# Seven-product units of a split-precision FFN: two units in a row share one tile for a quarter of their weights, and the later units' sums lie in the tile of the conditioning vectors

## The chip, the cores and the metric

One core of a Trainium2 chip runs the whole program in one launch. The time is device microseconds (us); three runs of the kernel before gave 1621.66, 1622.32 and 1625.24 us, median 1622.32.

## What is computed

The reference is a two-layer transformer over 256 latent and 256 context tokens, width 1024, in float32. The change touches its half feed-forward blocks (FFN, inner width 2816) and the vectors that modulate them:

```python
def half_ffn(h, shift, scale, gate, w_in, w_out, g, b):
    xm = modulate(h, shift, scale)
    a, u = jnp.split(xm @ w_in, 2, axis=-1)
    y = (jax.nn.silu(a) * u) @ w_out
    return post_norm(h, 0.5 * gate * y, g, b)

mod_lat = jnp.split((jax.nn.silu(c) @ ada_w[i] + ada_b[i])[:, None, :], N_MOD, axis=-1)
mod_ctx = jnp.split((jax.nn.silu(c_ctx) @ ada_w[i] + ada_b[i])[None, None, :], N_MOD, axis=-1)
```

Four such blocks are computed: first FFN of layer 0, attention, second FFN of layer 0, first FFN of layer 1, mLSTM, second FFN of layer 1. The change touches the second and third of the four.

## The kernel before

**Number format.** Every float32 operand of a matrix product is split into a high and a low part of type fp32r: `split` (lines 225 to 231) copies the value on ScalarE (ACT, line 226) into the high part, and VectorE (DVE, line 231) subtracts it from the value for the low part. `mm3` (line 240) then issues three matmuls, high by high, high by low, low by high; its `mm` is line 242 in the profile.

**Units.** The first product of an FFN, `w_in`, is done in 22 units of 128 columns of `a` and 128 of `u`. A plain unit streams 512 tokens through 16 weight blocks: 48 matmuls of 512 columns. In the two FFNs concerned (`FAST`, entries 1 and 2), units 9 to 21 are done by `fast_in` (line 643) with seven products of 2 by 2 blocks in place of eight: each product is 4 blocks deep and 256 tokens wide, so a unit is 84 matmuls of 256 columns. Its weights come by two DMAs of 512 KB (`raw`, line 211): `r0` holds the quarters a11 and a21, `r1` holds a12 and a22. DVE makes four sums s1 = a21 + a22, s2 = s1 + a11, s4 = s2 + a12, s3 = a11 + a21 (line 651), each 128 by 512, and `split` makes their high and low parts. The products run in the order a11, a12, s1, s2, a22, s4, s3. Between them ACT copies partial results out of PSUM (lines 676, 679, 681, 683): product 4 adds onto the bank that line 676 copies, product 6 onto that of line 679, product 7 onto that of line 681. At a unit's end come the sum at line 685, the Silu on ACT (line 686), lines 689 and 690 on DVE, and the split of the result into the unit's two tiles `gh`, `gl`.

**Order.** An FFN has two halves. Half 0 is units 0 to 10, then 8 output units (`unit_out`) that multiply by `w_out`; half 1 is units 11 to 21, then the other half of the outputs, of which the first four come ahead of the next norm. Each output unit is 33 matmuls of 512 columns, over eleven `gh`, `gl` pairs in their order, so the pair of unit 21 is read last. With the outputs run the dots that make the modulation vectors of later blocks: `ada_load` (line 353) fetches a row block of `ada_w`, `ada_dot` (line 359) multiplies it on DVE by both vectors silu(c), silu(c_ctx), 1220 ns each. These two vectors lie, repeated in all 128 partitions, in the tile `cb` of 2 by 1024 (`silu_c`, `silu_load` at line 306, `silu` at line 315). In the units 9 to 21 nothing reads `cb`; the output units of both halves do.

**Buffers.** Raw weights rotate through 3 tiles (`RAW`), split weights through 7 tiles of tag `w` (`WB`), each of which holds a high and a low part of 1024 columns; sums and other temporaries rotate through 6 tiles of tag `tmp`. A seven-product unit takes four `w` tiles, of which the first holds only the quarter a11 and stays half empty, and six `tmp` tiles: s1, s2, s4, s3 and its `a`, `u`.

**What sets the order on each engine.** The program is written in Python order; the framework's scheduler places the instructions of each engine in a fixed sequence of its own when the program is built, and adds the semaphores. Instructions passed through `pin` keep their written order. `fast_in`, `split`, `silu_load` and `silu` (as called here) are not pinned. All weight loads and the loads of `cb` are issued on SP's queue, one behind the other.

Of the kernel before, what the change touches and what calls it, by code (L numbers as in the profile page):

```python
# [27 lines left out]
NFH = 11  # L28
# [5 lines left out]
SH = 16  # L34
# [138 lines left out]
class Body:  # L173
# [75 lines left out]
    def x(self, d, g):  # L249
        return self.xh[:, d, g[0] : g[1]], self.xl[:, d, g[0] : g[1]]  # L250
# [350 lines left out]
    def fast_operands(self):  # L601

        self.flush()
        self.shut()
        self.cp = None
        st = self.open()
        n = ND // 2 * TL
        x = self.t([P, 6 * n], F32R, pool=st)
        self.t([P, FLIP], pool=st)
        self.made = [[x[:, (2 * i + p) * n : (2 * i + p + 1) * n].rearrange("p (k f) -> p k f", f=TL) for p in range(2)] for i in range(3)]  # L610
        self.first = {}

    def fast_sums(self, i):

# [28 lines left out]
    def fast_in(self, j, w_in, sh):  # L643

        nc, V, S = self.nc, self.nc.vector, self.nc.scalar
        half = 4 * P
        r0, r1 = (self.raw(w_in[2 * j + i]) for i in range(2))
        part = lambda x, i: x[:, i * half : (i + 1) * half]
        a11, a21, a12, a22 = part(r0, 0), part(r0, 1), part(r1, 0), part(r1, 1)
        s1, s2, s4, s3 = (self.tmp() for _ in range(4))  # L650
        add = lambda o, x, y: V.tensor_tensor(out=o, in0=x, in1=y, op=ALU.add)  # L651
        ws = [self.pair(sh=sh, n=half)] + [self.pair(sh=SH) for _ in range(3)]
        self.split(a11, *ws[0])
        self.split(r1, *ws[1])
        add(s1, a21, a22)
        add(s2, s1, a11)
        add(s4, s2, a12)
        add(s3, a11, a21)
        for i, x in enumerate((s1, s2, s4, s3)):
            self.split(x, *(part(y, i % 2) for y in ws[2 + i // 2]))  # L660
        w = {n: [part(x, i) for x in ws[p]] for n, p, i in (
            ("a11", 0, 0), ("a12", 1, 0), ("a22", 1, 1), ("s1", 2, 0), ("s2", 2, 1), ("s4", 3, 0), ("s3", 3, 1),
        )}
        of = lambda k0, g: lambda k: self.x(k0 + k, g)
        made = lambda i: lambda k: [x[:, k, :] for x in self.made[i]]

        def product(o, name, x, first, last):
            for k in range(ND // 2):
                c = slice(k * P, (k + 1) * P)
                self.mm3(o, [y[:, c] for y in w[name]], x(k), first and k == 0, last and k == ND // 2 - 1, group=False)  # L670

        x, yv, z = self.mm()[:, :TL], self.mm(), self.mm()[:, :TL]
        y, v = yv[:, :TL], yv[:, TL:]
        a, u = self.tmp(), self.tmp()
        product(x, "a11", of(0, LAT), True, False)
        S.copy(a[:, :TL], x)
        product(y, "a12", of(ND // 2, LAT), True, True)
        product(v, "s1", of(0, CTX), True, False)
        S.copy(u[:, TL:], v)
        product(x, "s2", made(0), False, False)  # L680
        S.copy(a[:, TL:], x)
        product(z, "a22", made(2), True, True)
        S.copy(u[:, :TL], z)
        product(v, "s4", of(ND // 2, CTX), False, True)
        V.tensor_tensor(out=a, in0=a, in1=yv, op=ALU.add)
        S.activation(a, a, AF.Silu)
        product(x, "s3", made(1), False, True)
        u2 = u.rearrange("p (n f) -> p n f", n=2)
        V.scalar_tensor_tensor(u2, x[:, None, :].broadcast_to([P, 2, TL]), -1.0, u2, ALU.mult, ALU.subtract)
        V.tensor_tensor(out=a, in0=a, in1=u, op=ALU.mult)  # L690
        gh, gl = self.gt[j] = tuple(self.t([P, self.gw], F32R, tag=k, bufs=self.gn, pool=self.gp) for k in ("gh", "gl"))
        self.split(a, gh, gl)

    def ffn(self, layer, s, gate, groups, side, start=None):
# [4 lines left out]
        with self.tc.tile_pool(name=f"ffn{li}", bufs=1) as gp:  # L699
# [6 lines left out]
            def unit_in(j, w, g, steps={}, ks=range(ND), ps=None):  # L706
                n = g[1] - g[0]
                pa, pu = ps or (self.mm(), self.mm())
                for k in ks:
                    for part, o in ((0, pa), (1, pu)):  # L710
                        self.mm3(o[:, :n], w(part_k(part, k)), self.x(k, g), k == 0, k == ND - 1)
                    self.steps(steps.get((j, k), ""))
                if ks[-1] < ND - 1:
                    return pa, pu
                self.ffn_g(j, pa, pu, g)
# [18 lines left out]
            for hf in range(2):  # L734
                js = list(range(hf * NFH, (hf + 1) * NFH))[0 if hf else done :]
                if hf == 0 and not start:
                    first = js[:LEAD]
                    ws = {j: Keep(self, [w_in[2 * j + i] for i in range(2)], lambda c: SH if c else SHR) for j in first}
                    assert len(self.running) == 1

                    k0, k1 = range(ND // 2), range(ND // 2, ND)
                    for j in first[:-1]:
                        unit_in(j, ws[j], LAT, LEADSTEP[li])
                    j = first[-1]
                    ps = unit_in(j, ws[j], LAT, ks=k0)
                    assert not self.running
                    pc = unit_in(first[0], ws[first[0]], CTX, ks=k0)
                    ws[j](ND)
                    unit_in(first[0], ws[first[0]], CTX, ks=k1, ps=pc)
                    unit_in(j, ws[j], LAT, ks=k1, ps=ps)  # L750
                    for j in first[1:]:
                        unit_in(j, ws[j], CTX)
                    for j in first:
                        call("in", j)
                    js = js[LEAD:]
                fast, sums = FAST[li]
                for j in js:
                    if j >= fast:
                        self.fast_in(j, w_in, SHR if j in (fast, NFH) else SH)
                    else:  # L760
                        unit_in(j, stream(j), allg)
                        if j >= LEAD + FAFTER:
                            self.fine = False
                    assert not self.running
                    if j <= sums:
                        call("in", j)
                    self.residual(2, self.pin)
                    if j == sums:
                        self.fast_operands()
                    if sums <= j < sums + 2:  # L770
                        self.fast_sums(j - sums)
                    if j == fast - 1:
                        self.fast_first()
                if not hf:
                    self.residual(len(self.later))
                w = Stream(self, [w_out[hf * NFH + i] for i in range(NFH)], lambda c, hf=hf: SHR if hf and c == (ND - TAIL) * NFH // ND else 0)
                body = ND - TAIL if hf else ND
                self.halves = []
                if hf and fast < NF:
                    self.shut()  # L780
                    self.cp = self.open()
                for d in range(body):
                    unit_out(hf, d, w, allg)
                    call("out", hf, d)
                self.halves = []
                if body < ND:
                    w = Keep(self, w.chunks, SH, w)
                    self.fine = True
                    for g in groups:
                        for d in range(body, ND):  # L790
                            unit_out(hf, d, w, g, TAILSTEP)
                            self.flush()
                    self.steps('B')
# [994 lines left out]
```

## Time and profile before

| | |
|---|---|
| runs | 1621.66, 1622.32, 1625.24 us; median 1622.32 us |
| the profiled execution's own time | 1621.19 us |
| its span, first to last instruction | 1619.4 us |
| mean granted TensorE clock | 0.999 |
| matmuls | 10424 |

The span is what the views below divide; 1.8 us of the execution's own time lie outside it. The profiled execution is 1.1 us under the median of the runs. Times in the views are us from the span's start.

### The profile page before, as it was taken

What the parts mean: (1) busy time and instruction counts of PE and PEld (TensorE: products, weight loads), DVE (VectorE), ACT (ScalarE), POOL (GpSimd) and SP (SyncE); (2) the same over time, 40 slices, a digit from 0 to 9 for tenths busy, and PEclk for the clock granted to TensorE, in tenths of its full rate; (3) what the DMA queues carried; (4) which work ended last, traced back from release to release, by engine and by line L of the source; (5) the groups of instructions that cost most, each with busy time, mean ns of one, the idle gap of its engine ahead of it and who ended that gap; (6) DMA issues with size and microseconds to landing.
All of it is one profiled execution on the core that took longest, in us unless ns stands there. A gap on an engine that the chain in (4) does not pass through costs nothing. (4 is left out here: it accounts for less than half of the span.)

```text
span 1619.4 us, 26945 instructions
## 1 busy us (share of the span) xinstructions
PE 1602.0 (99%) x10424; PEld 1452.0 (90%) x10424; DVE 1377.6 (85%) x2783; ACT 760.0 (47%) x1344; POOL 62.2 (4%) x77
## 2 busy tenths in 40 slices
PE   9999999999999999999999999999999999999998
PEld 7888888889988998889998998889999989999987
DVE  7789989878879879889996977789978968897697
ACT  6522132324676343515661444426642657566542
POOL 0000000001011200000000100000001000020000
PEclk9999999999999999999999999999999999999999
DMA  9667777642203343453254240752363332437552
GB/s 360 219 218 224 260 228 242 207 142 86 66 1 94 116 142 93 177 175 105 105 179 159 80 144 26 264 191 105 122 226 135 123 105 92 147 102 260 179 176 90
DMA packets 71648, 249.49 MB, mean 154 GB/s; under 512 B 7896, under 2 KB 10712, under 8 KB 71520
## 3 DMA queue, kind: packets, MB, share of 16 engines
q1 hardware_dynamic: 70944, 246.99, 46.2%
q8 instruction: 81, 1.33, 0.3%
q10 hardware_dynamic: 576, 0.79, 0.1%
q14 instruction: 47, 0.39, 0.1%
HBM read 246.69 MB, written 1.05 MB: 153 GB/s over the span
## 5 line engine op out<-in xcount | busy, mean ns | idle before, releaser
L242 PE MATMUL t<-t,t 128*128 128x256 f32 (+2 forms) x8484 | 1302.4, 314 | 5.5 <-DVE t L231 1.7
L242 PEld LDWEIGHTS t<-t,t 128*128 128x128 f32 x8484 | 1176.8, 188 | 117.0 <-DVE t L231 2.5
L226 ACT CAST t<-t 128x1024 fp32r<-128x1024 f32 (+4 forms) x573 | 436.4, 785 | 462.6 <-PE t L242 144.1
L231 DVE TENSOR_TENSOR t<-t,t 128x256 fp32r<-128x256 f32 (+3 forms) x792 | 516.5, 690 | 100.3 <-ACT t L226 98.5
L359 DVE SCALAR_TENSOR_TENSOR t<-t,t 128x1024 bf16<-128x1024 f32 x224 | 260.5, 1220 | 0.2 <-DMA t<-in_ada_w 0.2
L597 ACT ACTIVATE t<-t 128x256 f32<-128x256 f32 (+1 forms) x67 | 32.1, 485 | 108.9 <-PE t L242 107.9
L946 PE MATMUL t<-t,t 128*128 128x256 f32 (+1 forms) x256 | 79.5, 311 | 0.1
L948 PE MATMUL t<-t,t 128*128 128x256 f32 (+1 forms) x256 | 78.7, 307 | 0.1
L947 PE MATMUL t<-t,t 128*128 128x256 f32 (+1 forms) x256 | 78.3, 306 | 0.0
L728 DVE SCALAR_TENSOR_TENSOR t<-t,t,t 128x256 f32<-128x256 f32 x96 | 42.7, 478 | 32.3 <-PE t L242 32.2
L493 POOL TENSOR_TENSOR t<-t,t 128x256 f32<-128x256 f32 x30 | 23.0, 768 | 1106.4 <-ACT t L483 1105.0
L874 PE MATMUL t<-t,t 128*128 128x512 f32 (+1 forms) x300 | 60.5, 364 | 0.0
L874 PEld LDWEIGHTS t<-t,t 128*128 128x128 f32 x300 | 51.5, 189 | 8.9
L598 DVE TENSOR_TENSOR t<-t,t 128x256 f32<-128x256 f32 (+1 forms) x67 | 36.3, 545 | 25.5 <-ACT t L597 19.5
L651 DVE TENSOR_TENSOR t<-t,t 128x512 f32<-128x512 f32 x78 | 53.6, 687 | 3.0 <-DMA t<-in_ffn_in 2.2
L1475 PE MATMUL t<-t,t 128*128 128x512 f32 (+2 forms) x276 | 55.4, 356 | 0.0
L1475 PEld LDWEIGHTS t<-t,t 128*128 128x128 f32 (+1 forms) x276 | 44.9, 183 | 10.5 <-issue 0.4
L483 ACT ACTIVATE t<-t 128x256 f32<-128x256 f32 x72 | 26.3, 411 | 56.2 <-DVE t L476 56.2
L946 PEld LDWEIGHTS t<-t,t 128*128 128x128 f32 x256 | 48.4, 189 | 3.0 <-ACT t L550 0.3
L948 PEld LDWEIGHTS t<-t,t 128*128 128x128 f32 x256 | 48.1, 188 | 2.8 <-DVE t L551 0.3
L947 PEld LDWEIGHTS t<-t,t 128*128 128x128 f32 x256 | 48.1, 188 | 2.6
L550 ACT ACTIVATE t<-t,t 128x256 fp32r<-128x256 f32 x72 | 32.8, 502 | 30.1 <-DVE t L549 30.1
(209 smaller groups left out, 1117.5 us busy)
## 6 DMA issues: line engine op xcount, KB each, us to landing
t<-in_ffn_in SPq DMA_DIRECT2D x168, 512.0 KB, 4.0
t<-in_ada_w SPq DMA_DIRECT2D x138, 512.0 KB, 4.4
t<-in_ffn_out SPq DMA_DIRECT2D x66, 512.0 KB, 4.6
t<-in_ffn_last SPq DMA_DIRECT2D x22, 512.0 KB, 3.6
t<-in_att_in SPq DMA_DIRECT2D x12, 512.0 KB, 3.8
t<-in_att_out SPq DMA_DIRECT2D x8, 512.0 KB, 3.5
t<-in_ml_qk SPq DMA_DIRECT2D x8, 512.0 KB, 3.9
t<-in_ml_v SPq DMA_DIRECT2D x8, 512.0 KB, 4.0
```

What stands on the lines that cost most here:

```text
L226: self.behind(self.nc.scalar.copy(h, x))
L231: self.behind(self.nc.vector.tensor_tensor(out=ls, in0=xs, in1=hs.bitcast(F32), op=ALU.subtract))
L242: mm = lambda *k, **kw: self.nc.tensor.matmul(*k, skip_group_check=not group, **kw)
L359: ins = nc.vector.scalar_tensor_tensor(self.tmp().bitcast(BF16), r, 1.0, self.cb[:, v, :], ALU.mult, ALU.mult, accum_out=to)
L598: V.tensor_tensor(out=sl, in0=sl, in1=pu[:, :n], op=ALU.mult)
L651: add = lambda o, x, y: V.tensor_tensor(out=o, in0=x, in1=y, op=ALU.add)
L728: V.scalar_tensor_tensor(z, y[:, gg[0] - t0 : gg[1] - t0], gate()[:, v, d : d + 1], z, ALU.mult, ALU.add)
L874: pin(nc.tensor.matmul(o, gs[g], ws[k][w][:, i : i + n], start=k == k0 and g == w == 0, stop=k == k1 - 1 and g == 1,))
L946: mm(o, self.xh[:, k, c], wh, start=k == 0, stop=False)
L947: mm(o, self.xh[:, k, c], wl, start=False, stop=False)
L948: mm(o, self.xl[:, k, c], wh, start=False, stop=k == ND - 1)
L1475: mm = lambda *k, **kw: pin(nc.tensor.matmul(*k, **kw))
```

## The change

Three things are done in the two FFNs with seven-product units.

- Two units in a row share one `w` tile for their quarter a11: units 9 and 10, 11 and 12, 13 and 14 and so on; unit 21 opens one and uses half of it. The tile is kept in a list `quarter`.
- From unit 11 on, s1, s2, s4, s3 are written into `cb`, which has room for exactly four 512-column sums, in place of four `tmp` tiles; `split` is called twice, on 1024 columns each (s1 with s2, s4 with s3), in place of four times on 512.
- Behind unit 21 `cb` is loaded again and the Silu is applied again, ahead of the outputs of half 1.

```diff
-        self.first = {}
+        self.first, self.quarter = {}, []
...
-        s1, s2, s4, s3 = (self.tmp() for _ in range(4))
+        late = j >= NFH
+        sums = self.cb.rearrange("p v d -> p (v d)")
+        s1, s2, s4, s3 = (part(sums, i) if late else self.tmp() for i in range(4))
         add = lambda o, x, y: V.tensor_tensor(out=o, in0=x, in1=y, op=ALU.add)
-        ws = [self.pair(sh=sh, n=half)] + [self.pair(sh=SH) for _ in range(3)]
+        if not self.quarter:
+            p = self.pair(sh=sh)
+            self.quarter = [[part(x, i) for x in p] for i in range(2)]
+        ws = [self.quarter.pop(0)] + [self.pair(sh=SH) for _ in range(3)]
         self.split(a11, *ws[0])
         self.split(r1, *ws[1])
         add(s1, a21, a22)
         add(s2, s1, a11)
         add(s4, s2, a12)
         add(s3, a11, a21)
-        for i, x in enumerate((s1, s2, s4, s3)):
-            self.split(x, *(part(y, i % 2) for y in ws[2 + i // 2]))
+        if late:
+            for i in range(2):
+                self.split(self.cb[:, i, :], *ws[2 + i])
+        else:
+            for i, x in enumerate((s1, s2, s4, s3)):
+                self.split(x, *(part(y, i % 2) for y in ws[2 + i // 2]))
...
                 if hf and fast < NF:
                     self.shut()
                     self.cp = self.open()
+                    self.silu_load()
+                    self.silu()
```

## Rows read from the trace of the kernel before

**Rows 1.** The page, busy time of each engine over the span.
```profile
PE 1602.0 (99%) x10424; PEld 1452.0 (90%) x10424; DVE 1377.6 (85%) x2783; ACT 760.0 (47%) x1344; POOL 62.2 (4%) x77
```

**Rows 2.** Busy time by stretch: units 9-10, units 11-21, outputs; then the other FFN.
```profile
core 0: us, PE busy (x) PEld busy (x) DVE busy (x) ACT busy (x) POOL busy (x), PEclk, DMA share, GB/s
656.20:677.40 21.20, 20.01 (x170) 19.54 (x169) 19.22 (x31) 15.14 (x30) 0.00 (x0) 1.00 0.45 147
...
737.30:842.30 105.00, 105.00 (x926) 104.81 (x925) 100.62 (x152) 69.96 (x131) 0.00 (x0) 1.00 0.37 127
842.30:872.00 29.70, 29.70 (x134) 24.54 (x133) 21.27 (x48) 8.91 (x11) 0.00 (x0) 1.00 0.63 229
1007.30:1027.50 20.20, 19.78 (x170) 19.34 (x169) 19.09 (x30) 15.11 (x30) 0.00 (x0) 1.00 0.48 152
1087.40:1192.30 104.90, 104.90 (x926) 104.77 (x925) 100.79 (x152) 70.14 (x132) 0.00 (x0) 1.00 0.37 129
```

**Rows 3.** TensorE by stretch: units 12, 14, the other FFN's 12, then two equal stretches.
```profile
746.94:756.46 9.52, 9.52 (x87) 1.00 0.34 114
...
765.98:775.74 9.76, 9.76 (x87) 1.00 0.33 112
...
1097.04:1106.73 9.69, 9.69 (x87) 1.00 0.38 117
...
661.80:668.20 6.40, 6.40 (x56) 1.00 0.41 157
790.00:796.40 6.40, 6.40 (x59) 1.00 0.37 112
```

**Rows 4.** Groups by line and shape, units 9 and 10, 656.2 to 677.4 us.
```profile
L242 PE MATMUL t<-t,t 128*128 128x256 f32 x168 | 20.2, 280 | 1.2 <-DVE t L231 1.1
...
L651 DVE TENSOR_TENSOR t<-t,t 128x512 f32<-128x512 f32 x5 | 3.4, 687 | 1.6 <-DMA t<-in_ffn_in 1.6
```

**Rows 5.** ACT in order of time, units 13 and 14, 764 to 778 us.
```profile
768.80 1.05 ACT L226 CAST t<-t 128x1024 fp32r<-128x1024 f32 x1 [0.70 <-DMA t<-in_ffn_in]
769.76 0.36 ACT L676 COPY t<-t 128x256 f32<-128x256 f32 x1
...
775.12 1.15 ACT L226 CAST t<-t 128x512 fp32r<-128x512 f32 x2
```

**Rows 6.** DVE in order of time, the same stretch.
```profile
764.88 1.89 DVE L231 TENSOR_TENSOR t<-t,t 128x512 fp32r<-128x512 f32 x3
...
771.63 1.41 DVE L651 TENSOR_TENSOR t<-t,t 128x512 f32<-128x512 f32 x2
773.00 0.69 DVE L231 TENSOR_TENSOR t<-t,t 128x512 fp32r<-128x512 f32 x1
773.61 0.69 DVE L651 TENSOR_TENSOR t<-t,t 128x512 f32<-128x512 f32 x1
```

**Rows 7.** Groups by line and shape, units 11 to 21, 737.3 to 842.3 us.
```profile
L231 DVE TENSOR_TENSOR t<-t,t 128x512 fp32r<-128x512 f32 x64 | 42.2, 686 | 0.0
L226 ACT CAST t<-t 128x512 fp32r<-128x512 f32 x63 | 38.0, 622 | 15.5 <-DVE t L651 13.8 <-DVE t L690 0.7
...
L231 DVE TENSOR_TENSOR t<-t,t 128x1024 fp32r<-128x1024 f32 x14 | 17.1, 1222 | 1.5 <-ACT t L226 1.3
L226 ACT CAST t<-t 128x1024 fp32r<-128x1024 f32 x15 | 15.8, 1051 | 6.7 <-DMA t<-in_ffn_in 4.3 <-DMA t<-in_ffn_out 2.4
```

**Rows 8.** DVE in order of time, start of unit 11.
```profile
735.46 1.42 DVE L651 TENSOR_TENSOR t<-t,t 128x512 f32<-128x512 f32 x2
```

**Rows 9.** Sources 315 and 306: ACT's idle time ahead of the Silu; the vectors' landing.
```profile
  DMA t<-in_c: 12.7, 1
...
DMA to landing us min/median/max: 3.8/4.3/4.7
```

**Rows 10.** ACT in order of time, end of unit 21.
```profile
841.50 1.05 ACT L226 CAST t<-t 128x1024 fp32r<-128x1024 f32 x1 [2.07 <-DMA t<-in_ffn_out]
```

**Rows 11.** DVE in order of time, the last low parts of unit 21 among pieces of `w_out`.
```profile
846.86 2.03 DVE L231 TENSOR_TENSOR t<-t,t 128x256 fp32r<-128x256 f32 x5
```

## The prediction, made before the kernel was run

> **What bounds the kernel now.** First the page's busy times: TensorE (PE) is busy 99% of the span, VectorE (DVE) 85%, ScalarE (ACT) 47% [rows 1]. A busy PE says little alone, so next come the stretches with seven-product units, at a granted clock of 1.00 throughout, the 2.4 GHz level [rows 2]. One undisturbed unit takes 9.52 us [rows 3], 113.3 ns for each of its 84 matmuls, and eleven of them make 104.7 us; units 11 to 21 take 105.0 us in one FFN and 104.9 in the other [rows 2]. So at most 0.3 and 0.2 us of waiting lie in the stretch where the change does most. Units 9 and 10 have 21.2 and 20.2 us [rows 2] where two undisturbed units take 19.04: 2.2 and 1.2 us lost. All that this change could win where it acts, at PE's present pace, is thus 3.3 + 0.5 = 3.8 us, 0.23% of the time. I take 0.2%, 3.2 us, as what a measurement of this kernel can tell from no change.
>
> Then what the other engines do there. DVE is busy 100.6 of 105.0 us in units 11 to 21, 96%, ACT 70.0 [rows 2]: the feed of weights is close behind PE, and what it does on time matters more than how much.
>
> **Part 1: four splits of 512 become two of 1024 (units 11 to 21).** By busy time DVE saves 4 x 686 - 2 x 1222 = 300 ns a unit and ACT 4 x 622 - 2 x 1051 = 386 ns [rows 7]; over 22 units 6.6 and 8.5 us. The instructions overlap their neighbours, so less of it is room: three subtractions of 512 take 1.89 us in a row, some 0.60 each [rows 6]. None of it lies on PE's path as long as PE waits for none of these parts, so I cost it at nothing. The cover is that the splits run a unit ahead.
>
> What does wait on the feed is small. In unit 14 PE loses 9.76 - 9.52 = 0.24 us, in the other FFN's unit 12 0.17 [rows 3]. The cause shows on ACT: the 1024-wide copy of a raw tile waits 0.70 us for its DMA, and behind it on ACT stands the copy of line 676, from 769.76 to 770.12 [rows 5]. Product 4 adds onto that bank; it is due three products into unit 14, 765.98 + 3 x 1.36 = 770.06. That copy comes 0.06 late, plus the hand-over. The DMA was late because its raw tile comes free only when DVE has made the sums, and DVE puts a subtraction, 0.6 us, between the sums s2 and s4 [rows 6]. With 1024-wide splits that subtraction cannot start until ACT has copied s1 and s2 together, 1.05 us, so the four sums should follow each other; the raw tile then comes free some 0.6 us earlier in every unit, and both waits should go: -0.4 us. If the scheduler puts the 1.22 us subtraction there instead, the tile is free 0.5 us later and the waits stay or grow; I take -0.4 with 0 as the other end here and price the worse end with the slower rival.
>
> The new cost is that s1 is ready only with s2. It bites at unit 11, which has no unit of the same kind ahead. Its first two sums are ready at 735.46 + 1.42 = 736.9 [rows 8]; a copy of 1.05 and a subtraction of 1.22 [rows 7] put the low part at 739.2; product 3 needs it at 737.4 + 2 x 1.36 = 740.1. If the other two sums and the two output sums of line 728 go ahead on DVE (some 2.1 us), it is 1.1 us late. Bounds 0 and +1.1 in each FFN; I take +0.1 each, near the end without a wait, since DVE must stand idle for ACT's 1.05 us anyway and can do two of those four in it.
>
> The Trainium skill (Perfetto Trace Analysis, Optimizing Scalar/DVE Operations) says that large operations help a saturated engine, but that if ACT or DVE is not saturated and causes bubbles elsewhere, breaking instructions up lets work finish sooner. By its second half the merge would cost at unit 11 what the upper bound says, 2.2 us in all; by its first half, with DVE at 96%, nothing. I go by the rows' 0.9 us of room.
>
> **Part 2: the sums lose their rotating tiles.** They now lie in one place, so a unit's sums must wait for the last unit's splits. Before, the splits of unit 14's sums stand on DVE at 764.88 for 1.89 us and the next unit's first sum at 771.63 [rows 6]: 4.9 us between. No wait, 0 us. [...] At unit 11 the sums must also follow the last dot that reads the vectors; both are on DVE, where the sums come behind the dots already.
>
> **Part 3: the shared quarter.** Two units take seven `w` tiles in place of eight. In units 9 and 10 PE waits 1.1 us, and that for a DVE subtraction; DVE in turn waited 1.6 us for a weight DMA [rows 4]. A free `w` tile mends neither, and these units keep their `tmp` sums. So 0, with bounds -3.3 (all waits there go) and 0. The other side: a new pair's tile is held until the first product of the pair's second unit ends.
>
> **Part 4: the vectors are made again.** Per FFN two DMAs on SP and two Silus on ACT, beside two waits: the DMAs wait for unit 21's last split, and all weight loads stand behind them on SP; the Silus wait for the DMAs, and the copies of unit 21 stand behind them on ACT. The same load ahead of this FFN landed 4.3 us after issue, and ACT stood 12.7 us idle for it [rows 9], at a place where PE did not need ACT. Two 1024-wide ACT instructions cost 2 x 1.05 = 2.1 us [rows 7]. At the end of unit 21 ACT is idle 2.07 us in one piece, for a DMA [rows 10]: room for both. If they land badly, the last pair `gh`, `gl` is late: outputs start at 842.3, at 29.70/134 = 0.22 us a matmul [rows 2], and the low part is read by the 32nd, at 849.2; the DVE group that holds it ends at 848.9 [rows 11]. So 0.3 us of slack at least, and a bound of 2.1 - 0.3 = 1.8 us per FFN from work alone. The weight loads have more cover: a 1024-column chunk feeds 24 matmuls, 5.3 us. Bounds 0 and +1.8 each; I take +0.1 each, by the idle 2.07 us. The dots that need the vectors come after the first output unit, 33 x 0.22 = 7.3 us later, against 4.3 + 2.1 = 6.4 us for load and Silu.
>
> **Sum.** -0.4 + 0.2 + 0 + 0 + 0.2 = 0.0 us on the profiled execution's 1621.2; its own runs' median lies 1.1 us higher, so the forecast is **1622.3 us**, no change.
>
> **Rivals.**
> *Faster: the waits of units 9 and 10 go as well,* because a freed `w` tile or another order on DVE brings the sums of unit 10 early. For it: 3.3 us are really lost there. Against: the wait shown is for a DMA. Time: 1622.3 - 3.3 - 0.4 = 1618.6.
> *Slower: PE falls into its slower pace in units 11 to 21.* After the waits in unit 9, 56 matmuls fit in 6.40 us where 59 fit in an undisturbed stretch, with no wait between [rows 3]: 5% slower, and it lasted until the next wait. If a wait in unit 11 or 12 leaves PE so, ten units lose 0.05 x 9.52 = 0.48 us each, 4.8 us in one FFN. Against: after the waits of units 12 and 14 the next stretch is at full pace (59 in 6.40). It decides where s1's low part misses 740.1 or line 676's copy its time. Time: 1627.
> *Slower: the reload holds ACT.* ACT reaches the first Silu before the DMA has landed and stands there. Price: 2.1 us of work and up to 4.3 - 2.07 = 2.2 of waiting, less 0.3: 4.0 at most, some 1.5 to 2 us likely, per FFN. It decides where the Silu stands ahead of line 683's copy or of the copy into `gh`. Time: 1625.3 to 1626.3, or inside 0.2% if one FFN is spared.
> *The sharing makes a wait of its own.* The copy of a later unit's a11 is made early: it is one of the two copies at 775.12 to 776.27 [rows 5], while unit 15's first product ends at 775.74 + 1.36 = 777.1. If it must wait for that, ACT stands 0.8 to 1.4 us in every second unit, and line 676 is late as in unit 14: 0.3 to 0.5 us in ten units, 1626. Other `w` tiles are free at that time, which speaks against it.
>
> **How the numbers follow.** Forecast 0.66 (all within 0.2%); faster 0.08; pace 0.08; reload 0.12, half of it past 0.2%; sharing 0.06. Faster by over 0.2%: 0.08; within: 0.66 + 0.06 = 0.72; slower: 0.08 + 0.06 + 0.06 = 0.20. The range takes in the reload and the sharing, and leaves out most of the two outer cases: 1619.2 to 1626.5.
>
> **What would show it.** Right: in units 11 to 21 two 1024-wide copies and subtractions per unit in place of four of 512; the four sums in one block on DVE; 104.7 us for each eleven units; units 9 and 10 at 21 and 20 us; two more Silus at line 315 per FFN with PE at full pace at the start of the outputs. Wrong: a PE wait in unit 11 on the 1024-wide subtraction; fewer than 59 matmuls in 6.40 us anywhere in units 11 to 21; idle ACT ahead of line 315 with PE waiting behind it; units 9 and 10 near 19 us.

## The result, and the profile after

The changed kernel is **slower**: median 1628.08 us (1623.85 to 1629.53, 9 runs) against 1621.25 us before (1620.02 to 1625.24, 9 runs), ratio 1.0035 with interval [1.0025, 1.0046]. The forecast of no change was wrong, and the median lies past the end of the range, 1626.5 us. The profiled execution took 1629.53 us, the slowest of its nine; its span is 1627.7 us, 8.3 more than before.

The page first, for [rows 1]:

```profile
span 1627.7 us, 26880 instructions
...
PE 1608.3 (99%) x10424; PEld 1456.5 (89%) x10424; DVE 1372.0 (84%) x2739; ACT 755.0 (46%) x1304; POOL 62.3 (4%) x77
```

DVE has 44 instructions and 5.6 us less, ACT 40 and 5.0 us, as the merge of the splits said. PE has the same 10424 matmuls and is busy 6.3 us longer, at the same granted clock. So less was done, and it took longer. The stretches say where (columns as in [rows 2], and the same stretches):

```profile
657.10:678.90 21.80, 20.10 (x170) 19.50 (x169) 18.73 (x30) 14.67 (x29) 0.00 (x0) 1.00 0.46 164
738.80:846.90 108.10, 106.00 (x925) 105.22 (x924) 98.57 (x130) 69.02 (x113) 0.00 (x0) 1.00 0.42 136
...
1011.70:1032.20 20.50, 20.06 (x170) 19.62 (x170) 18.48 (x29) 14.82 (x29) 0.00 (x0) 1.00 0.48 161
1092.10:1200.30 108.20, 108.16 (x926) 107.96 (x925) 97.45 (x128) 68.36 (x112) 0.00 (x0) 1.00 0.44 137
```

Units 11 to 21 went from 105.0 to 108.1 us in the second FFN and from 104.9 to 108.2 in the third: 6.4 of the 8.3 us. Units 9 and 10 have 0.6 and 0.3 more, the start up to unit 9, which the change does not touch, 0.9. The two 3 us are not of one kind: PE was idle 2.1 us in the second FFN and next to never in the third.

**Second FFN: waits for copies out of PSUM.** The line numbers are moved by nine: the copies after a11, s1, s2, a22 (676, 679, 681, 683 before) are now 685, 688, 690, 692. PE's sequencer in the list of waits, 738 to 847 us (total, times, longest):

```profile
ACT t L315 <- DMA t<-in_c: 4.0, 1, 4.0
...
PEld t L242 <- ACT t L690: 2.3, 2, 1.9
...
PEld t L242 <- ACT t L685: 0.4, 1, 0.4
...
PEld t L242 <- ACT t L688: 0.2, 1, 0.2
```

The longest is in unit 20. ACT there in order of time:

```profile
830.12 0.37 ACT L688 COPY t<-t 128x256 f32<-128x256 f32 x1 [0.52 <-PE t L242]
834.54 1.06 ACT L315 ACTIVATE t<-t 128x1024 f32<-128x1024 f32 x1 [4.04 <-DMA t<-in_c]
835.50 0.35 ACT L690 COPY t<-t 128x256 f32<-128x256 f32 x1
835.75 1.05 ACT L226 CAST t<-t 128x1024 fp32r<-128x1024 f32 x1
836.70 0.38 ACT L692 COPY t<-t 128x256 f32<-128x256 f32 x1
836.97 1.07 ACT L315 ACTIVATE t<-t 128x1024 f32<-128x1024 f32 x1
```

then SP's queue and PE over the same time:

```profile
828.38 2.08 SPq L306 DMA_DIRECT2D t<-in_c  x2
```

```profile
835.91 2.33 PE L242 MATMUL t<-t,t 128*128 128x256 f32 x18 [1.74 <-ACT t L690]
```

The first Silu of the reload stands between unit 20's copies after s1 and after s2. SP issues the load from 828.38 on, ACT stands 4.04 us for its landing, and the copy of line 690, possible from about 831.3 us on (the end of product 4, unit 20 having started at 825.84), goes behind it. Product 7 adds onto that bank and waits for it.

**Third FFN: a wait of 0.2 us, and then a slower pace.** The whole list of the waits of PE's sequencer from 1092 to 1200 us is one line:

```profile
PEld t L242 <- ACT t L688: 0.2, 1, 0.2
```

It is in unit 13. Behind it PE runs at a slower pace up to the outputs. Seventy microseconds of it, without a wait, in the changed kernel, then seventy in the kernel before:

```profile
1125.00:1195.00 70.00, 70.00 (x597) 70.00 (x596) 62.32 (x82) 44.02 (x72) 0.00 (x0) 1.00 0.41 124
```

```profile
1115.00:1185.00 70.00, 70.00 (x620) 70.00 (x619) 68.98 (x106) 48.05 (x92) 0.00 (x0) 1.00 0.34 121
```

597 matmuls where 620 fitted, at a granted clock of 1.00 (2.4 GHz) in both: by their starts one each 117.8 ns against 113.3, 9.89 us a unit against 9.52, so 0.37 us a unit. Eight units and the rest of unit 13 make 3.1 us. Where the 0.2 us come from stands on ACT, and then on DVE, in order of time:

```profile
1115.36 2.52 ACT L226 CAST t<-t 128x1024 fp32r<-128x1024 f32 x3 [1.44 <-DVE t L653]
1117.78 0.36 ACT L688 COPY t<-t 128x256 f32<-128x256 f32 x1
```

```profile
1111.10 0.69 DVE L653 TENSOR_TENSOR t<-t,t 128x512 f32<-128x512 f32 x1 [0.86 <-DMA t<-in_ffn_in]
1111.71 0.68 DVE L653 TENSOR_TENSOR t<-t 128x512 f32<-128x512 f32 x1
1112.31 0.68 DVE L694 TENSOR_TENSOR t<-t,t 128x512 f32<-128x512 f32 x1
1112.91 1.22 DVE L231 TENSOR_TENSOR t<-t,t 128x1024 fp32r<-128x1024 f32 x1
1114.04 0.68 DVE L698 SCALAR_TENSOR_TENSOR t<-t,t 128x512 f32<-128x512 f32 x1
1114.64 0.68 DVE L653 TENSOR_TENSOR t<-t,t 128x512 f32<-128x512 f32 x1
```

DVE makes s1 at 1111.10, after 0.86 us of waiting for its DMA, then s3 (its row has one input tile), and s2 only at 1114.64, behind a 1024-wide subtraction and two instructions of the unit before. The merged copy of s1 and s2 cannot start without s2; it opens a row of three copies on ACT, 2.52 us, and line 688 comes behind them, done at 1118.14. Unit 13 starts at 1111.19, so product 6 is due five products later, at 1111.19 + 5 x 1.36 = 1117.99.

### The profile page after: what moved, and what is told of

It is laid out like the page before. It is cut to its first block, busy times and chain, and to the rows that moved or that the text cites. A ratio compares the mean times of both kernels' runs of the same rounds, so it can differ in the third digit from the quotient of the medians.

```text
span 1627.7 us, 26880 instructions
## 1 busy us (share of the span) xinstructions
PE 1608.3 (99%) x10424; PEld 1456.5 (89%) x10424; DVE 1372.0 (84%) x2739; ACT 755.0 (46%) x1304; POOL 62.3 (4%) x77
## 5 line engine op out<-in xcount | busy, mean ns | idle before, releaser
L226 ACT CAST t<-t 128x1024 fp32r<-128x1024 f32 (+3 forms) x529 | 429.2, 835 | 478.9 <-PE t L242 155.8
```

The lines of the kernel that those rows point to most:

```text
L226: self.behind(self.nc.scalar.copy(h, x))
```

## The experiments

**The theory (T),** as it read after the first batch. PE's losses come of ACT's fixed row. The copies out of PSUM after products 1, 3 and 4 are due 2.72 us, two products, after the product that they copy. They come late when a copy of weights that waits for its DMA or for its sum, a wide copy, or the reload's Silu stands ahead of them. A short wait can also leave PE in its slower pace. **The rival**: the shared tile, or the one place for the sums, holds the work itself.

In the tables "lost" is what PE lost in units 11 to 21, worked out from the starts of the 84 matmuls of each unit less 113.3 ns each, in the second and in the third FFN of the one profiled execution. Times are medians over all runs of a kernel; each batch of kernels ran on one chip with its own runs of the kernel before.

### First batch: parts of the change

Sharing alone, on the kernel before:

```diff
-        self.first = {}
+        self.first, self.quarter = {}, []
...
-        ws = [self.pair(sh=sh, n=half)] + [self.pair(sh=SH) for _ in range(3)]
+        if not self.quarter:
+            p = self.pair(sh=sh)
+            self.quarter = [[part(x, i) for x in p] for i in range(2)]
+        ws = [self.quarter.pop(0)] + [self.pair(sh=SH) for _ in range(3)]
```

> Sharing the quarter's tile alone, sums and splits as before, nothing loaded again. Theory A (the loss comes from 1024-wide copies on ACT ahead of the copies out of PSUM, from the reload, and from the slower pace of PE that a wait leaves behind): units 11 to 21 stay at 104.7 to 105.2 us in both FFNs, the time within 1.5 us of before. Theory B (the shared tile makes the waits): units 11 to 21 at 107 us or more in both, 5 us slower than before. Either may show 0.3 to 0.8 us more in units 9 and 10.

The sums in `cb`, two splits of 1024 and the reload, without the sharing (the diff of the change less the lines above):

> The changed kernel without the sharing: each unit has its own tile for its quarter; sums in the vectors' tile, two splits of 1024, reload. Theory A: slower than before by 4 to 7 us, like the changed kernel, with PE waits on the copies out of PSUM and on the one behind the Silu. Theory B: within 1.5 us of before.

The change without the reload:

```diff
-                    self.silu_load()
-                    self.silu()
```

> The changed kernel without the reload: the vectors are not made again, so the dots after unit 21 multiply by what the sums left there; their work is the same. Theory A: the 2.0 us wait in unit 20 of the first of the two FFNs goes; 0.4 to 0.8 us waits in units 13 to 17 and the slower pace (0.38 us a unit) can stay; 2 us faster than the changed kernel, 4 us slower than before. If the reload is the whole cause: at the time of before.

The change with four splits of 512 from `cb`:

```diff
-            for i in range(2):
-                self.split(self.cb[:, i, :], *ws[2 + i])
+        for i, x in enumerate((s1, s2, s4, s3)):
+            self.split(x, *(part(y, i % 2) for y in ws[2 + i // 2]))
```

> The changed kernel with four splits of 512 in place of two of 1024; sums still in the vectors' tile, sharing and reload kept. Theory A: no wait on the copies out of PSUM in units 11 to 19, full pace there (9.52 us a unit); the reload's wait at unit 20 can stay, 0 to 2 us an FFN: 0 to 3 us slower than before. If the one place for the sums or the sharing is the cause: as slow as the changed kernel.

The kernel before had 1622.3 us here; the changed kernel's row is from its own runs. Ratios are taken over all runs of a batch and are not quotients of the medians.

| kernel | us | ratio to before | lost, 2nd and 3rd FFN |
|---|---|---|---|
| before | | | 0.31, 0.24 |
| changed | 1628.08 | 1.0035 [1.0025, 1.0046] | 3.46, 3.51 |
| sharing alone | 1626.94 | 1.0022 [1.0009, 1.0034] | 2.39, 3.28 |
| sums and reload alone | 1628.91 | 1.0042 [1.0028, 1.0055] | 4.29, 1.94 |
| change, no reload | 1625.1 | 1.0016 [1.0006, 1.0026] | 3.10, 0.11 |
| change, 512 splits | 1624.0 | 1.0008 [0.9998, 1.0018] | 1.14, 1.92 |

The row of sharing alone falsified the theory as it stood then, with the 1024-wide copies as the cause: sharing alone has neither these nor a reload, and loses most of what the change loses. Its units 11 to 21 take 107.0 and 108.0 us, as the rival had set for it. But to the sums and reload alone the rival gave 1.5 us at most, and they lose about as much as the whole change. The kernel with 512 splits agrees with neither: it is faster than the changed kernel, against the rival, and PE waits in units 16 and 17 of its second FFN and 13 to 15 of its third, where the theory had no wait. The trace of sharing alone names the same kind of wait as before, PE's sequencer on the copy after a11 (line 679 there), second FFN:

```profile
PEld t L242 <- ACT t L679: 1.1, 3, 0.6
```

and ACT in unit 14:

```profile
768.43 1.05 ACT L226 CAST t<-t 128x1024 fp32r<-128x1024 f32 x1 [1.11 <-DMA t<-in_ffn_in]
769.39 0.36 ACT L679 COPY t<-t 128x256 f32<-128x256 f32 x1
```

This is the pattern of [rows 5], the copy of `r1` waiting for its DMA ahead of the copy out of PSUM, 0.4 us worse. Part of that is PE coming earlier: unit 14 starts at 765.20 in place of 765.98, since units 9 and 10 lost less in this execution, and the copy of `r1` at 768.43 in place of 768.80. No ACT instruction of this kernel waits for PE to free a weight tile in those units, so the shared tile is not what holds. With 512 splits the same copy is late behind two 512-wide copies (ACT, unit 16, where it is due at 789.4):

```profile
788.27 1.12 ACT L226 CAST t<-t 128x512 fp32r<-128x512 f32 x2
789.30 0.36 ACT L681 COPY t<-t 128x256 f32<-128x256 f32 x1
```

What all of them have in common is seen in ACT's row itself. Read from the traces, units 12 to 20 of the second FFN; A, V, X, Z are the copies after a11, s1, s2, a22, S a Silu, W a 1024-wide copy into a weight tile, h a 512-wide copy:

```
before          AWhVhXhZhhhSW AhVhhXhZhhSW (the same in units 13 to 19) AhVhhXhZhWSW
sharing alone   AWhhVhXhZhhhS AWhVhXhhZhhSW AhhVhhXhZhSW AhVhhXhZhhSW AhhVhhXhZhSW AhVhhXhZhhSW AhhVhhXhZhSW AhVhhXhZhhSW AhVhhXhZhWSW
changed         AhhVXWZWWS AhVWXWZhWSh AhWVWXZWS AWhWVXhZWhSW AWhVXWZWSW AhVXhhZWWS AWhVXWZWWS AhVXhZWWS AWhVSXWZSWSW
```

The kernel before has settled into one row for seven units, with one or two copies of 512 ahead of V, X and Z, and two of them, the Silu and one W ahead of the next unit's A. The others change from unit to unit: sharing alone has by turns two copies of 512 and one between A and V, and the changed kernel has up to three copies ahead of V and, in unit 20, the Silu between V and X.

What one copy more between A and V does is seen where both kernels are level, in unit 16, which starts at 785.26 in both. DVE there, before and then with sharing alone:

```profile
788.55 1.82 DVE L231 TENSOR_TENSOR t<-t,t 128x1024 fp32r<-128x1024 f32 x2
790.29 1.41 DVE L651 TENSOR_TENSOR t<-t,t 128x512 f32<-128x512 f32 x2
```

```profile
788.57 2.42 DVE L231 TENSOR_TENSOR t<-t,t 128x1024 fp32r<-128x1024 f32 x3
790.91 1.41 DVE L651 TENSOR_TENSOR t<-t,t 128x512 f32<-128x512 f32 x2
```

A second copy brings a third subtraction ahead of the next sums. The sums come 0.6 us later, and SP issues the load of weights that waits for them 0.6 us later too. The copy of `r1` ahead of unit 17's copy after a11 comes 0.97 us later, and PE, which began unit 17 at 794.78 in both kernels, waits 0.33 us. ACT before and then with sharing alone:

```profile
796.85 1.05 ACT L226 CAST t<-t 128x1024 fp32r<-128x1024 f32 x1 [0.15 <-DMA t<-in_ffn_in]
```

```profile
797.82 1.05 ACT L226 CAST t<-t 128x1024 fp32r<-128x1024 f32 x1 [0.23 <-DMA t<-in_ffn_in]
```

The same row can also get by. Without the reload unit 13 of the third FFN has the row that it has in the changed kernel, but s1 did not wait for its DMA there, and the copy after s1 is done at 1115.74, 0.8 us before product 6 is due (the unit starts at 1109.73), where in the changed kernel it was 0.15 late. DVE and then ACT:

```profile
1108.70 0.68 DVE L653 TENSOR_TENSOR t<-t,t 128x512 f32<-128x512 f32 x1
```

```profile
1115.38 0.36 ACT L688 COPY t<-t 128x256 f32<-128x256 f32 x1
```

The reload is not the reason: the last kernel of the second batch keeps it, and its copy was 0.8 us early there too. So the row sets how near PE is to a wait, and the landing of a DMA decides; a loss read from one execution need not be in every other.

### Second batch: the order written down

A helper puts one ACT instruction behind another by an edge without a semaphore. In the first three kernels the copy of the next unit's `r1` goes behind A, those of s1 and s2 behind V, those of s4 and s3 behind X; in the last two the reload's Silus go behind unit 21's copy into `gh`.

```diff
+    def after(self, ins, last):
+        if last is not None:
+            edge = mybir.DependencyInfo(mybir.DependencyClass.NoSync, mybir.DependencyReason.DATA)
+            self.tc.add_manual_dep(ins.ins, last.ins.name, edge, reason="behind a copy")
...
-        self.split(r1, *ws[1])
+        p, self.prev = self.prev, {}
+        self.split(r1, *ws[1], p.get("a"))
...
-        S.copy(a[:, :TL], x)
+        self.prev["a"] = S.copy(a[:, :TL], x)
...
-                    self.silu()
+                    self.silu(lambda ins: self.after(ins, self.last))
```

> The kernel before (sums in tmp, a w tile per quarter), with three orders on ACT written down: the copy of the next unit's r1 stands behind the copy after a11, the copies of s1 and s2 behind the copy after s1, those of s4 and s3 behind the copy after s2. Theory T (TensorE's waits come of the place that copies out of PSUM have in ACT's row): the two waits of units 12 and 14 in the second FFN go, their stretch of units 11 to 21 is at most 104.8 us in each FFN, and the kernel is 0 to 1.5 us faster than before. Rival (the waits come of the shared tile and of the one place for the sums, which this kernel does not have): the order is worth nothing here, within 0.5 us of before. If the order makes sums late, units 11 to 21 get longer and T's cure is wrong.

> Sharing alone (the first experiment) with the same three orders on ACT. Theory T: the waits on the copy after a11 (2.0 us in 6 in the trace of sharing alone) and the slower pace behind them go, units 11 to 21 take 104.7 to 105 us in each FFN, time within 1 us of before. Rival (the shared tile itself makes TensorE wait): units 11 to 21 stay 2 to 3 us longer in each FFN and the kernel stays 3 to 5 us slower than before.

> The whole change with the same three orders, and both Silus of the reload behind unit 21's copy into gh. Theory T: no wait on a copy out of PSUM over 0.2 us, units 11 to 21 take 104.7 to 105 us in each FFN, time from 3 us under to 1 us over the kernel before. Rival (sums in one place: the next unit's sums wait until the copies and subtractions of this one have left cb, and TensorE waits behind them): units 11 to 21 stay about 3 us longer in each FFN, the kernel 4 to 6 us slower than before.

> The change with one order alone: both Silus of the reload stand behind unit 21's copy into gh. Theory T: of the 3.5 us that units 11 to 21 lost in the second FFN the 2.0 us in unit 20 go, the rest and the third FFN's 3.3 us stay: about 2 us faster than the changed kernel, 3 to 4.5 us slower than before. Rival (the reload is only one of several things late in unit 20): the wait moves to another copy and the time stays at the changed kernel's, 5.7 us slower than before.

| kernel | us (before: 1622.51) | ratio to before | lost, 2nd and 3rd FFN |
|---|---|---|---|
| before, ordered | 1621.95 | 0.9991 [0.9982, 1.0] | 0.07, 0.07 |
| sharing alone, ordered | 1623.47 | 1.0002 [0.9994, 1.0011] | 0.11, 0.11 |
| changed, ordered | 1622.23 | 0.9997 [0.9988, 1.0005] | 0.58, 1.09 |
| changed, Silus moved only | 1625.4 | 1.002 [1.001, 1.003] | 1.24, 0.11 |

T held in the main. The kernel before has no wait left in these units, though its 0.6 us do not tell T from the rival by time. Sharing keeps its shared tile and loses 0.11 us an FFN once the row is right; the whole change is level with before, but with two waits over the 0.2 us that T allowed. With the Silus alone the 2.0 us of unit 20 are gone and the waits of units 14 to 17 stay; its third FFN, against T, was undisturbed in the profiled execution, which at 1621.97 us was the fastest of its eleven.

The 0.58 and 1.09 left in the changed and ordered kernel lie in unit 21, where no later unit's copies are ordered. ACT there, second FFN, and PE's only wait in the third:

```profile
838.77 1.57 ACT L232 CAST t<-t 128x1024 fp32r<-128x1024 f32 x2 [3.08 <-DMA t<-in_ffn_out]
840.25 0.36 ACT L698 COPY t<-t 128x256 f32<-128x256 f32 x1
```

```profile
PEld t L251 <- ACT t L698: 0.9, 1, 0.9
```

Two copies of `w_out` wait 3.08 us for their DMA, and the copy after s1 behind them.

### Third batch: that last wait, and the slower pace by itself

The copies of the first three row blocks of `w_out` go behind unit 21's V, X and X:

```diff
...
+                    self.order = [self.prev[k] for k in "vxx"]
                     self.silu_load()
...
-        self.split(r, h, l)
+        self.split(r, h, l, self.order.pop(0) if self.order else None)
```

> The whole change with the orders of the third kernel of the batch before, and one more: the copies of the first three row blocks of w_out, which stood in ACT's row ahead of unit 21's copy after s1 and waited 3.1 and 3.7 us for their DMA, stand behind unit 21's copies after s1 and after s2. Theory T: the waits of unit 21 (0.5 us in the second FFN, 0.9 us in the third) go, units 11 to 21 are at 104.8 us in each FFN, the time is 1 to 2 us less than with the other orders alone: level with the kernel before or up to 2 us faster. Rival: w_out's copies now come late for the first output unit, and what unit 21 gains is lost there.

It took 1620.93 us, before 1621.64, ratio 0.9992 [0.9983, 1.0001]. Units 11 to 21, both FFNs:

```profile
737.50:842.40 104.90, 104.90 (x926) 104.90 (x925) 97.06 (x129) 64.90 (x108) 0.00 (x0) 1.00 0.38 125
1087.40:1192.20 104.80, 104.80 (x926) 104.80 (x925) 96.00 (x127) 63.49 (x107) 0.00 (x0) 1.00 0.37 125
```

DVE has 97.1 us of work there where it had 100.6 [rows 2], ACT 64.9 in place of 70.0, and PE takes its least time, as T expected.

The pace was tried on the ordered kernel before, which has no wait in these units:

```diff
+        self.reps = [7, 8, 9, 10, 11, 12]
...
-        self.prev["a"] = S.copy(a[:, :TL], x)
+        for _ in range(self.reps.pop(0) if j in (12, 15, 18) else 1):
+            self.prev["a"] = S.copy(a[:, :TL], x)
```

> The kernel before with the three orders on ACT (in whose trace units 11 to 21 have no wait at all), and work on ACT added at three places of each of the two FFNs: in units 12, 15 and 18 the copy after a11 is done 7, 8, 9 times in the second FFN and 10, 11, 12 times in the third, each at about 0.26 us, so that product 4, due 2.72 us after product 1, waits for the last. Theory (a short wait of TensorE by itself can leave it at the slower pace of 117.75 ns a matmul until its next wait): waits of 0 to 2 us in units 12, 15, 18, and behind some of them, not all, units of 9.89 us instead of 9.52 up to the next wait. Rival (the slower pace comes of something else that the changed kernel has, its 1024-wide copies, the shared tile or its DMAs): every unit behind the waits is back at 113.3 ns, 9.52 us.

All six places made PE wait, 0.7 to 1.9 us. Behind the three of the second FFN PE went on at full pace. In the third it went on at the slower pace behind units 12 and 15; in unit 18 it came back to the full pace and fell again within two products, behind a gap of 0.08 us. Sixteen microseconds behind unit 12's wait, without a wait in them, in the second FFN and in the third:

```profile
753.00:769.00 16.00, 16.00 (x144) 16.00 (x143) 15.30 (x25) 11.30 (x22) 0.00 (x0) 1.00 0.32 107
1116.00:1132.00 16.00, 16.00 (x138) 16.00 (x138) 15.36 (x25) 10.17 (x21) 0.00 (x0) 1.00 0.21 74
```

In the third FFN units 13, 14, 16, 17 and 19 to 21 lost 0.37 us each with no wait of their own. This kernel has no shared tile and no 1024-wide copy of sums, so the rival falls: waits bring the slower pace without anything of the change. The time, one run, was 1633.33 us.

### Last: is the change worth anything once ordered?

The ordered kernel before and the ordered changed kernel of the third batch, on one chip:

> The kernel before with the three orders, beside the whole change with all its orders on one chip. Theory (the change's own work lies beside TensorE, all its loss was order): the two are within 1 us of each other in median, both 0.5 to 2 us under the kernel before. Rival (the 44 instructions less on DVE and 40 less on ACT are worth something once the order is right): this one is 1 us or more slower than the other.

> The whole change with all its orders, beside the kernel before with the three orders on one chip. Theory: within 1 us of it. Rival (less work on DVE and ACT is worth something): 1 us or more faster than it.

Before 1621.83 us; ordered 1622.08 (0.9996 [0.9987, 1.0005]); changed and ordered 1621.44 (0.9994 [0.9985, 1.0003]). They are 0.6 us apart, and neither can be told from before, so the 0.5 to 2 us hoped for both did not show. Each came out 0.04 to 0.09% under before in both its batches (0.9991 and 0.9996; 0.9992 and 0.9994), which may be a gain of about 1 us, but no batch shows it. There is no version here that beats the kernel before by more than its measurement is uncertain.

## Why the prediction was wrong

- **The step that failed** is in part 1: "None of it lies on PE's path as long as PE waits for none of these parts, so I cost it at nothing. The cover is that the splits run a unit ahead." The splits do run ahead. But they stand in the same row of ACT as the copies out of PSUM, which do not: these are due 2.72 us after their product. Anything that waits ahead of them takes from that, and PE pays. Part 1 saw this in unit 14 [rows 5], worked out a lateness of 0.06 us plus the hand-over, and took it for one late DMA to be cured by faster sums, not for the margin of every unit. Taking the order of ACT and DVE as given, with some instructions shortened, was the error: a new program got a new row.
- **Part 1, the two waits to go, -0.4 us.** The two on the copy after a11 went, and others came, one of them in unit 14 itself, on the copy after s2: 3.46 us lost in the second FFN, and the wait of 0.2 us with what followed in the third. "The four sums should follow each other" was wrong; the other end given there, the 1.22 us subtraction between the sums, is what the DVE rows of unit 13 show, and its cost was left to a rival. Unit 11, +0.1 us with up to 1.1: near enough, it lost 0.04, as before the change.
- **Part 2, 0 us.** Right in itself: with every order written down (the changed kernel of the third batch), sums in one place lose 0.20 and 0.11 us, less than the 0.31 and 0.24 of the kernel before.
- **Part 3, 0 us.** The tile costs next to nothing (0.11 us an FFN when ordered, against 0.07 without it), but sharing as built cost 3.6 us (ratio 1.0022). The rival "the sharing makes a wait of its own" gave 1626 for it, and 1626.94 was measured, but that is luck: in that kernel no copy waits for PE to leave a weight tile. In the changed kernel some do, 7.1 us in five units of the third FFN, and PE waits behind none of these. It was the row again: with one copy more between A and V the sums come later, and so does W, which waits for its DMA ahead of A. Units 9 and 10 did not gain; over the traces of this study they lost 1.2 to 2.9 us in the second FFN with and without the change, so the 0.6 us more are not laid to it.
- **Part 4, +0.1 us for each reload.** In the second FFN it was 2.0; in the third 0, where the Silu stood in the same place and ACT waited 1.8 us for the load. The price of the rival (1.5 to 2 us, the Silu ahead of a copy out of PSUM with its DMA still under way) was right, and so was its mechanism; its place was not. I looked for it at the end of unit 21 [rows 10]. But `cb` is free as soon as unit 21's sums are split, a unit ahead by the sentence of part 1, and so the Silu came into unit 20, where ACT has no 2.07 us to spare. Of the rest, right: no wait at the outputs.
- **The slower pace**, given 0.08, carried most of the third FFN's loss. The forecast had 5% and 0.48 us a unit from a short stretch; it is 3.9% and 0.37 us.
- **The Trainium skill's rule** (Perfetto Trace Analysis, Optimizing Scalar/DVE Operations), that breaking up the instructions of an unsaturated ACT or DVE may help where they make another engine idle, was held to concern unit 11 alone. The change with 512 splits took 1624.0 us against 1628.08 with 1024, on different chips; their intervals do not meet. By that the rule held in the other units too, though 512 splits do not end the waits: their row loses 1.14 and 1.92 us. With the orders written down, 1024-wide splits took no longer than the kernel before.

Left open: why the scheduler keeps one row before and changes it in each unit after; whether the order on DVE, which the edges on ACT moved with it, would have done alone; which of the three orders does most, as they were not tried one by one; and what decides whether a wait leaves PE at the slower pace.

## What to carry to other kernels

Where copies out of PSUM share an in-order engine with copies that wait for DMAs, give each of them its due time (here 2.72 us after its product) and ask what stands ahead of it; an edit that only removes work can still cost time by reordering that row. Compare the row of the engine unit by unit before and after the edit, and pin the few instructions that have a due time before judging the edit. An engine busy 46% of the span held up one busy 99%: its order was the cause and not its load, and the order on DVE had a part in it.

## What was not expected of the hardware

A stream of matmuls of 256 columns has two paces at the same granted clock of 1.00, 113.3 and 117.8 ns each, and a short wait can leave PE in the slower one until a later wait or until the 512-column outputs; once, in unit 20 of the kernel with sharing alone, it came back by itself. Of 48 gaps of over 0.02 us in units 11 to 21, over the fourteen traces, 11 were followed by twelve matmuls at the slower pace, 34 by twelve at or near the faster, 3 by another wait. Length did not decide: 0.2 us led to it in unit 13 of the changed kernel, and 2.0 us in unit 20 did not. Nor did it always take such a gap: in unit 14 of the changed kernel's second FFN ten matmuls ran at the slower pace behind none of over 0.02 us.
